# Second norm in place, transposes ahead of the Strassen sums, four gate/up products among them, fixed engine orders and ordered down loads

## The chip, the cores and the metric

The kernel runs on one core of one Trainium2 chip. The metric is device time in microseconds (us), median of several runs. Engines: PE (TensorE), DVE (VectorE), ACT (ScalarE), POOL (GpSimd) and SP (SyncE, which here only issues DMAs). All data are float32; a matmul operand is split into a high and a low part (float32r), and a product is the sum of three matmuls: high x high, high x low, low x high.

## The reference

One encoder layer on 1024 tokens of width 1024, with a hidden width of 2816. The Hyena mixer up to `y` is not touched.

```python
def rmsnorm(x, g):
    return x * lax.rsqrt(jnp.mean(x * x, axis=-1, keepdims=True) + RMS_EPS) * g

def swiglu(x, w_gate, w_up, w_down):
    return (jax.nn.silu(x @ w_gate) * (x @ w_up)) @ w_down

mixed = y @ w_out + b_out            # end of hyena_mixer(rmsnorm(x, norm_mix))
x = x + mixed
x = x + swiglu(rmsnorm(x, norm_ffn), w_gate, w_up, w_down)
return rmsnorm(x, norm_final)
```

## The kernel before

The tokens stand in eight tiles `x1[0..7]` of 128 tokens by 1024 channels. Four stages matter here.

**Out projection** (`out_mm`, L535). Blocks are done in pairs (m, m+4), first the left 512 output columns of all pairs (`po00` to `po03`), then the right 512 (`po10` to `po13`): 24 matmuls of 128x512 for a block and half. DVE adds the result onto `x1` (L551), and POOL adds the bias `bo` to the whole tile (L628).

**Second norm** (`norm2`, L570). For a pair, ACT squares both tiles (L576), DVE works out the reciprocal root in five tiny steps around an ACT square root (L133 to L138) and scales into a new tile `xm` (L579), and POOL's queue stores `x1` to DRAM (`X1D`, L559). gate/up are Strassen-Winograd products of 2x2 blocks, so DVE forms the sums of token and channel halves (`tt`, L588 to L591); PE transposes the four quarters and the sums (`tpa` to `tpd`, L598), 28 transposes of 128x128 a pair; ACT and DVE split the result into the operands `u2`, `T1`, `T2` and `T3`.

**gate/up** (`pair`, `unit`, `product`, L677). 11 pairs of a gate and an up unit; a unit has 7 products of 12 matmuls, named a, f, g, e, b, d, c, with right operands B11, T2, T3, T1, B21, T4, B22. Its weights come in two SP loads (`wgr`, `wur`). The hidden values and their sums (`g`, `sx`) are stored in `HD[0..6]` by POOL's queue; those of the last pair are "held" and stored by SP.

**Down product** (`product2`, L808). Seven products p1, p5, p6, p3, p7, p2, p4 of 132 matmuls. `operands` loads hidden blocks (`hrp`, POOL's queue), splits them into `hop`, and splits the weights `wd` into `wop`. Three slots of `hop` and `wop` take turns; one of each is the slot of `g` (tag `inv`) and of `sx` (`whl0`). DVE forms the weight sums `t1` (L856), `t2` (L861, L834) and `t4` (L867). Then come the last norm and the output stores.

The Tile framework puts the instructions of every engine in order by a simulated time line; a tile waits for its tag's slot, and a DMA from SP waits for its lane (eight of them).

Of the kernel before, what the change touches and what calls it, by code (L numbers as in the profile page):

```python
# [73 lines left out]
def hyena_ffn_kernel(ctx: ExitStack, tc: tile.TileContext, a: dict, out: bass.AP):  # L74
# [462 lines left out]
    def out_mm(pt, h, js):  # L537
        for k in range(NB):
            for q, j in enumerate(js):
                th, m = divmod(j, 4)  # L540
                for ti, (yi, wi) in enumerate(TERMS):
                    T.matmul(  # L542
                        pt[:, q * 512 : (q + 1) * 512],
                        u2[yi][th][:, k, m * P : (m + 1) * P],
                        wos[h][k // 2][wi][:, k % 2, :],
                        start=(k == 0 and ti == 0),
                        stop=(k == NB - 1 and ti == len(TERMS) - 1),
                    )
        for q, j in enumerate(js):
            d = x1[j][:, h * 512 : (h + 1) * 512]  # L550
            V.tensor_tensor(d, d, pt[:, q * 512 : (q + 1) * 512], ALU.add)  # L551

# [18 lines left out]
    def norm2(m):  # L571
        js = PAIRS[m]
        xm = slot("whl0", f"xm{m}", (2, 1024))
        sq = small(f"sq{m}", 2, tag="sq", bufs=2)
        for q, j in enumerate(js):
            S.activation(xm[:, q], x1[j], AF.Square, accum_out=sq[:, q : q + 1])  # L576
        rs = rstd_of(sq, 2, f"rq{m}")
        for q, j in enumerate(js):
            V.scalar_tensor_tensor(xm[:, q], x1[j], rs[:, q : q + 1], gffn, ALU.mult, ALU.mult)  # L579
# [1 line left out]
        if m == 0:
            t_op("T1", "ab_g", ("gg0",))
            t_op("T2", "cr", ("fwd01",))
            t_op("T3", "whl1", ("hs", "wt"))
        b11, b21 = xm[:, 0, 0:512], xm[:, 0, 512:1024]
        b12, b22 = xm[:, 1, 0:512], xm[:, 1, 512:1024]
        tt = slot("inv", f"tt{m}", (3, 512))
        V.tensor_tensor(tt[:, 0], b12, b11, ALU.subtract)  # L588
        V.tensor_tensor(b12, b22, b12, ALU.subtract)
        V.tensor_tensor(tt[:, 1], b12, b11, ALU.add)  # L590
        V.tensor_tensor(tt[:, 2], b21, tt[:, 1], ALU.subtract)  # L591
        ms = slice(m * P, (m + 1) * P)

        def turn(nm, srcs):
            pt = cv_psum(f"{nm}{m}")
            for i, src in enumerate(srcs):
                for k in range(4):
                    T.transpose(  # L598
                        pt[:, i * 512 + k * P : i * 512 + (k + 1) * P],
                        src[:, k * P : (k + 1) * P],  # L600
                        ident,
                    )
            return pt

        def whole(pt, th):
            split(u2[0][th][:, :, ms], u2[1][th][:, :, ms], pt.rearrange("p (k m) -> p k m", k=NB))

        def part(pt, i, nm):
            src = pt[:, i * 512 : (i + 1) * 512].rearrange("p (k m) -> p k m", k=4)
            hi, lo = tops[nm]  # L610
            S.copy(hi[:, :, ms], src)
            n = 4 // len(lo)
            for x, l in enumerate(lo):
# [1 line left out]
                V.tensor_tensor(l[:, :, ms], src[:, ks], hi[:, ks, ms].bitcast(F32), ALU.subtract)
# [9 lines left out]
    for m in range(4):  # L625
        out_mm(po[m], 0, PAIRS[m])
        for j in PAIRS[m]:
            G.tensor_tensor(x1[j], x1[j], bo, ALU.add)  # L628
# [22 lines left out]
    def unit(i, w, nm):  # L651
        raw = []
        for kh in range(2):
            r = slot(RAW[n_raw[0] % 4], f"{nm}r{i}{kh}", (4, 256))
# [34 lines left out]
        V.tensor_tensor(s1, a21, a22, ALU.add)
# [6 lines left out]
        product(pd, "e", s1, "T1", True)
        product(pa, "b", a12, "B21", False)
        V.tensor_tensor(s4, a12, s2, ALU.subtract)
        return (pa, pd, dc_, uu), (
            lambda: product(pc, "d", a22, "T4", False),  # L700
            lambda: product(pd, "c", s4, "B22", False),
        )

    def quads(un, rest, out):
        pa, pd, dc_, uu = un
        V.tensor_tensor(out[:, 2], uu[:, 2], pd, ALU.add)
        for f in rest:
            f()
        u2b = uu[:, 1:2].broadcast_to([P, 2, 512])
        V.tensor_tensor(  # L710
            out[:, 0:2], u2b, dc_.rearrange("p (q c) -> p q c", q=2), ALU.add
        )
# [217 lines left out]
```

## Time and profile before

| | us |
|---|---|
| median of 3 runs (1321.77 to 1322.64) | 1322.37 |
| the profiled execution | 1314.3 |
| its span | 1312.5 |
| PE busy in the span | 1193.7 |
| DVE busy | 928.7 |
| ACT busy | 435.2 |
| POOL busy | 342.7 |

The profile is of one execution. Its span runs from the first to the last instruction. An idle time in brackets stands ahead of an instruction and names what ended it.

### The profile page before, as it was taken

The numbers are of one execution on the slowest core, as the hardware profiler recorded it, in microseconds if no ns is written. First come the engines' busy times: TensorE is split into PE (matmuls) and PEld (weight loads), VectorE is DVE, ScalarE is ACT, GpSimd is POOL, SyncE is SP. The second block draws the span as 40 slices with busy tenths as digits, with TensorE's granted clock in tenths as the row PEclk, the third lists the DMA queues.
The fourth block names the chain that finished last, engine by engine and source line by source line (L and its number), as shares of the span: only waits on it lengthen the run. The fifth ranks groups of instructions, "written<-read, shape, count | busy, mean of one in ns | idle before, by whom it ended". The sixth has DMA issues, their size and how long they took to land.

```text
span 1312.5 us, 14959 instructions
## 1 busy us (share of the span) xinstructions
PE 1193.7 (91%) x5726; PEld 987.1 (75%) x5726; DVE 928.7 (71%) x1342; ACT 435.2 (33%) x665; POOL 342.7 (26%) x311
## 2 busy tenths in 40 slices
PE   3899989998999778993999999999999967999996
PEld 3688878787888667883788888888888746778875
DVE  5546999989999997367576566666657553945567
ACT  6434332333333141124332333232333321424542
POOL 0023855755754581600010010110001100000100
PEclk9999999999999888996899999999999988999999
DMA  9343231331242353141132233333232595333332
GB/s 280 79 91 89 50 80 32 73 100 37 56 103 50 115 191 98 42 151 48 48 103 90 89 105 113 104 106 109 91 96 96 192 379 191 89 88 88 96 121 96
DMA packets 88808, 139.71 MB, mean 106 GB/s; under 512 B 6559, under 2 KB 57887, under 8 KB 88609
## 3 DMA queue, kind: packets, MB, share of 16 engines
q1 hardware_dynamic: 72929, 83.44, 20.0%
q0 software_dynamic: 15808, 55.32, 14.6%
q8 instruction: 45, 0.74, 0.2%
q14 instruction: 26, 0.21, 0.0%
HBM read 94.43 MB, written 31.72 MB: 96 GB/s over the span
## 4 chain that ended last, share of the span: by engine, by line
PE 62%; DVE 25%; DMA 6%; issue 3%; POOL 2%; ACT 2%; SPq 0%; DVEq 0%; POOLq 0%; ACTq 0%
PE wgdc L677 9%; PE wudc L677 9%; PE z L111 8%; PE bx L808 7%; PE wgab L677 7%; PE wuab L677 7%; PE po L542 5%; PE by L808 3%; PE bz L808 2%; DMA wd<-in_ffn_w_down_dram 2%; DVE ss L438 2%; DVE l L383 1%; DVE vz L309 1%; DVE x L309 1%; DMA whl<-wt 1%
## 5 line engine op out<-in xcount | busy, mean ns | idle before, releaser
L111 PE MATMUL z<-uh,whl 128*128 128x512 f32 x768 | 223.3, 404 | 12.2 <-DVE x L309 3.7
L111 PEld LDWEIGHTS z<-uh,whl 128*128 128x128 f32 x768 | 145.6, 193 | 45.0 <-ACT uh L100 3.8
L808 PE MATMUL bx<-wop,hop 128*128 128x512 f32 x528 | 130.2, 403 | 21.8 <-ACT wop L100 13.0
L808 PEld LDWEIGHTS bx<-wop,hop 128*128 128x128 f32 x528 | 100.8, 193 | 49.1 <-ACT wop L100 14.2
L111 PE MATMUL z<-ul,whl 128*128 128x512 f32 x384 | 128.0, 404 | 0.0
L559 POOL DMA_DIRECT2D hd<-g x40 | 21.5, 540 | 373.0 <-DVE g L727 246.2
L101 DVE TENSOR_TENSOR hop<-hrp,hop 128x1024 fp32r<-128x1024 f32 (+1 forms) x42 | 47.5, 1133 | 57.9 <-ACT hop L100 57.9
L542 PE MATMUL po<-wohl,uh 128*128 128x512 f32 x256 | 84.4, 411 | 1.7 <-POOL wohl L101 1.7
L111 PEld LDWEIGHTS z<-ul,whl 128*128 128x128 f32 x384 | 73.6, 193 | 15.9 <-issue 0.5
L559 POOL DMA_DIRECT2D hrp<-hd x42 | 22.3, 531 | 223.4 <-DVE hop L101 179.1
L100 ACT CAST hop<-hrp 128x1024 fp32r<-128x1024 f32 (+1 forms) x42 | 40.8, 976 | 102.5 <-PE bx L808 69.0
L808 PE MATMUL by<-wop,hop 128*128 128x512 f32 x264 | 63.4, 394 | 0.8 <-DVE wop L101 0.5
L542 PEld LDWEIGHTS po<-wohl,uh 128*128 128x128 f32 x256 | 49.9, 197 | 13.4 <-POOL wohl L101 1.9
L808 PEld LDWEIGHTS by<-wop,hop 128*128 128x128 f32 x264 | 49.2, 188 | 13.5 <-DVE wop L101 2.0
L393 PE MATMUL pg<-hw,fwd 128*128 128x128 f32 x256 | 49.6, 277 | 7.7 <-DVE hw L381 7.1
L542 PE MATMUL po<-wohl,ul 128*128 128x512 f32 x128 | 51.8, 407 | 1.4 <-DVE ul L101 1.4
L165 POOL DMA_DIRECT2D whl<-wt x24 | 20.9, 871 | 122.3 <-ACT whl L164 122.3
L392 PE MATMUL pg<-hw,fwd 128*128 128x128 f32 x256 | 49.7, 276 | 0.0
L393 PEld LDWEIGHTS pg<-hw,fwd 128*128 128x128 f32 x256 | 39.3, 193 | 8.6 <-DVE hw L381 7.3
L163 ACT CAST whl<-wt 128x1024 fp32r<-128x1024 f32 x24 | 25.0, 1043 | 56.5 <-PE z L111 33.2
L101 DVE TENSOR_TENSOR wop<-wd,wop 128x512 fp32r<-128x512 f32 x55 | 36.2, 686 | 6.2 <-ACT wop L100 4.5
L392 PEld LDWEIGHTS pg<-hw,fwd 128*128 128x128 f32 x256 | 39.4, 193 | 0.3
(661 smaller groups left out, 2972.1 us busy)
## 6 DMA issues: line engine op xcount, KB each, us to landing
hrp<-hd POOLq DMA_DIRECT2D x35, 512.0 KB, 3.9
wt<-in_hy_w_in_dram SPq DMA_DIRECT2D x24, 512.0 KB
whl<-wt POOLq DMA_DIRECT2D x24, 512.0 KB, 4.5
wgr<-in_ffn_w_gate_dram SPq DMA_DIRECT2D x22, 512.0 KB
wur<-in_ffn_w_up_dram SPq DMA_DIRECT2D x22, 512.0 KB
wd<-in_ffn_w_down_dram SPq DMA_DIRECT2D x44, 256.0 KB
hd<-g POOLq DMA_DIRECT2D x40, 256.0 KB, 2.5
hd<-sx POOLq DMA_DIRECT2D x30, 256.0 KB, 2.6
```

The lines of the kernel that those rows point to most:

```text
L100: S.copy(hi, src)
L101: (eng or V).tensor_tensor(lo, src, hi.bitcast(F32), ALU.subtract)
L111: T.matmul(pt[:, h * 512 : (h + 1) * 512], w[wi], u2[ui][h][:, k, :], start=first and ti == 0, stop=last and ti == len(TERMS) - 1,)
L163: S.copy(whl[:, 0], wt)
L309: V.scalar_tensor_tensor(o, i, w, o, ALU.mult, ALU.add)
L392: T.matmul(o, fwd[r][:, j, :], hw[:, j, 0, :], start=True, stop=False)
L393: T.matmul(o, fwd[2 * r][:, jj, :], hw[:, jj, 1, :], start=False, stop=True)
L438: V.tensor_tensor(ss[:, 1], gg[:, 0], gg[:, 1], ALU.subtract)
L542: T.matmul(pt[:, q * 512 : (q + 1) * 512], u2[yi][th][:, k, m * P : (m + 1) * P], wos[h][k // 2][wi][:, k % 2, :], start=(k == 0 and ti == 0),
L559: G.dma_start(dst, src)
L677: T.matmul(pt, t[:, wi, k, :], b(k)[ui], start=first and k == 0 and ti == 0, stop=k == 3 and ti == len(TERMS) - 1, skip_group_check=not first,
L808: T.matmul(pt, ho[:, hi_, x, q * P : (q + 1) * P], wo_[:, wi, x, :], start=fresh and first and x == 0 and ti == 0, stop=last and x == n - ...
```

## The change

It has five parts.

1. The bias is no longer added by POOL's arithmetic: eight DMAs from POOL's queue add it onto `x1` in memory as each tile is loaded.
2. The left half of each block is squared when it is added (`x1_half`). SP stores each half in place of POOL's whole tile. The right half goes block by block in the order 0, 4, 1, 5, 2, 3, 6, 7. `normed` scales `x1[j]` in place, which has to follow its store.
3. `turned` transposes the normed block itself, eight transposes, 64 in all. The sums are taken afterwards from PSUM (`top_left`, `top_sums`), and three of the splits go to POOL.
4. Products a and b of both units of pair 0 stand between the last transposes, with operands split by ACT and POOL (`pre`, `pg`, `pu`). PE, DVE and ACT take the written order there.
5. SP issues in written order from the pair loop on. The down product's weight sums are formed in place (`less`), with one operation each for p5, p6, p7 and p4.

In the program's order on PE this is the stretch around the last transposes, before; the names are tile (`tp…`, `wgab`) and its operands:

```order
L598 MATMUL tpd1_4016<-ident_65,tt1_3979 128x128 x4
L598 MATMUL tpd1_4016<-ident_65,xm1_3964 128x128 x4
L598 MATMUL tpa2_4098<-ident_65,xm2_4078 128x128 x8
L598 MATMUL tpb2_4109<-ident_65,tt2_4093 128x128 x4
L598 MATMUL tpb2_4109<-ident_65,xm2_4078 128x128 x4
L598 MATMUL tpc2_4123<-ident_65,tt2_4093 128x128 x4
L598 MATMUL tpd2_4130<-ident_65,tt2_4093 128x128 x4
L598 MATMUL tpd2_4130<-ident_65,xm2_4078 128x128 x4
L598 MATMUL tpa3_4212<-ident_65,xm3_4192 128x128 x8
L677 MATMUL wgab0_4262<-uh0_61,wga0_4264 128x512
```

and in the change, on PE at block 2's transposes, between matmuls of the out projection:

```order
L549 MATMUL po14_4032<-wohl13_3570,uh0_61 128x512 x2
L549 MATMUL po14_4032<-wohl13_3570,ul0_63 128x512
L602 MATMUL tp2_4133<-ident_65,x12_3535 128x128 x8
L549 MATMUL po16_4158<-wohl10_3555,uh1_62 128x512 x2
L549 MATMUL po16_4158<-wohl10_3555,ul1_64 128x512
```

Before, the transposes of pair 2 and the first of pair 3 stand in a row with no other matmul between them; now each block's eight stand behind the next block's 24 matmuls.

On ACT, in the change, these rows follow block 5's sums (`jq` is the square of a half, `rq` the square root, `pre` the early operands of pair 0):

```order
L100 CAST uh_62<-tp_4057 128x4x128
L100 CAST pre<-wgr_4096 128x512
L100 CAST pre<-wur_4100 128x512
L563 ACTIVATE jq_4143,sq_3590<-x_3538 128x512
L590 ACTIVATE rq_4146<-rq_4146 128x1
L610 CAST uh_61<-tp_4133 128x8x128
L611 COPY x_3535<-tp_4133 128x1024
```

The two casts of loaded weights stand ahead of the square of block 3 (`x_3538`); the second of them reads the up unit's load `wur`.

On SP, around the held stores of the last pair (`hd`), before:

```order
L97 DMA wd9_7137<-in_ffn_w_down_dram 128x512 x2
L97 DMA hd1_3570<-g10_6875 128x512
L97 DMA hd3_3572<-g10_6875 128x512
L97 DMA wd9_7137<-in_ffn_w_down_dram 128x512 x2
L97 DMA y1t_7138<-xd0_3576 128x512
L97 DMA y1t_7138<-xd1_3577 128x512
L97 DMA y1t_7138<-xd2_3578 128x512
L97 DMA y1t_7138<-xd3_3579 128x512
L97 DMA wd1_7131<-in_ffn_w_down_dram 128x512
L97 DMA hd4_3573<-sx10_7125 128x512
L97 DMA wd3_7133<-in_ffn_w_down_dram 128x512
L97 DMA hd6_3575<-g10_6875 128x512
```

and in the change:

```order
L97 DMA wd7_7167<-in_ffn_w_down_dram 128x512 x2
L97 DMA wd9_7168<-in_ffn_w_down_dram 128x512 x2
L97 DMA hd0_3575<-g10_6906 128x512
L97 DMA hd1_3576<-g10_6906 128x512
L97 DMA hd3_3578<-g10_6906 128x512
L97 DMA hd4_3579<-sx10_7156 128x512
L97 DMA hd5_3580<-sx10_7156 128x512
L97 DMA hd6_3581<-g10_6906 128x512
L97 DMA hd2_3577<-sx10_7156 128x512
L97 DMA wd0_7161<-in_ffn_w_down_dram 128x512
```

The held stores stood among the loads of `wd` and of the residual (`y1t`), near the end of them; now they stand together behind the first eleven loads of `wd`.

The core of the diff:

```diff
-    bo = slot("hs", "bo")
-    load(bo, a["hy_b_out"].partition_broadcast(P)[:, 0, :])
+    bo = a["hy_b_out"].partition_broadcast(P)[:, 0, :]
     for j in range(NB):
         t = slot(x1_tags[j], f"x1{j}")
         load(t, xv[:, j, :])
+        G.dma_start(t, bo, accum_op=ALU.add)
...
+    def x1_half(j, h, o):
+        c = slice(h * 512, (h + 1) * 512)
+        V.tensor_tensor(x1[j][:, c], x1[j][:, c], o, ALU.add)
+        S.activation(
+            slot("junk", f"jq{j}{h}", (512,)), x1[j][:, c], AF.Square, accum_out=sq2[j][:, h : h + 1]
+        )
+        load(X1D[j][:, c], x1[j][:, c])
...
-    def norm2(m):
...
-        for q, j in enumerate(js):
-            V.scalar_tensor_tensor(xm[:, q], x1[j], rs[:, q : q + 1], gffn, ALU.mult, ALU.mult)
-            store(X1D[j], x1[j])
...
-        whole(turn("tpa", (b11, b21)), 0)
-        pt = turn("tpb", (tt[:, 1], b12))
-        part(pt, 0, "T2")
-        part(pt, 1, "T3")
-        pt = turn("tpc", (tt[:, 0],))
-        part(pt, 0, "T1")
-        whole(turn("tpd", (tt[:, 2], b22)), 1)
...
+    def normed(j):
...
+        for h in range(2):
+            d = x1[j][:, h * 512 : (h + 1) * 512]
+            V.scalar_tensor_tensor(d, d, r0, gffn[:, h * 512 : (h + 1) * 512], ALU.mult, ALU.mult)
+
+    def turned(j):
+        pt = cv_psum(f"tp{j}")
+        for k in range(NB):
+            T.transpose(pt[:, k * P : (k + 1) * P], x1[j][:, k * P : (k + 1) * P], ident)
+        return pt.rearrange("p (k m) -> p k m", k=NB)
...
+    def top_left(m, pt):
+        ms = cols_of(m)
+        S.copy(u2[0][0][:, :, ms], pt)
+        S.copy(x1[m].rearrange("p (k m) -> p k m", k=NB), pt)
+        V.tensor_tensor(u2[1][0][:, :, ms], pt, u2[0][0][:, :, ms].bitcast(F32), ALU.subtract)
+
+    def top_sums(m, pt):
...
+        S.copy(t3, b12)
+        V.tensor_tensor(t1, b12, left[:, 0], ALU.subtract)
+        V.tensor_tensor(t2, b22, t1, ALU.subtract)
+        V.tensor_tensor(t3, b22, t3, ALU.subtract)
+        part("T2", t2, V)
+        V.tensor_tensor(t4, left[:, 1], t2, ALU.subtract)
+        part("T3", t3, G)
+        part("T1", t1, G)
+        split(u2[0][1][:, 0:4, ms], u2[1][1][:, 0:4, ms], t4, G)
+        split(u2[0][1][:, 4:8, ms], u2[1][1][:, 4:8, ms], b22)
...
+    def w_early(t, src):
+        split(t[:, 0], t[:, 1], src, G)
+        return t
...
+    with tc.manual_schedule(
+        engines={mybir.EngineType.PE, mybir.EngineType.DVE, mybir.EngineType.Activation}
+    ):
+        for n, j in enumerate(seq):
...
+            for k in range(NB):
+                out_mm(o, 1, j, k)
...
+            if 1 <= n <= 6:
+                turn(seq[n - 1])
+            x1_half(j, 1, o)
+            if n == 6:
+                post(3)
+            normed(j)
+            if 1 <= n <= 5:
+                post(seq[n - 1])
+            if n == 4:
+                ug, uu_ = Unit(0, wg, "wg"), Unit(0, wu, "wu")
+                pre = slot("whl0", "pre", (2, 2, 4, P), F32R)
+                for x, u in enumerate((ug, uu_)):
+                    w_early(pre[:, x], u.a11)
...
+        ug.sums(G)
+        ug.p1(pre[:, 0])
+        ug.p1_out()
+        pg = w_early(slot("fwd2", "pg", (2, 4, P), F32R), ug.a12)
+        turn(6)
+        uu_.p1(pre[:, 1])
+        post(6)
+        pu = w_early(slot("xz", "pu", (2, 4, P), F32R), uu_.a12)
+        uu_.p1_out()
+        turn(7)
+        ug.p2(pg)
+        post(7)
+        uu_.p2(pu)
+        ug.early = {"f": w_op("wg0f", ug.s[:, 1])}
...
+    ctx.enter_context(tc.manual_schedule(engines={mybir.EngineType.SP}))
...
-    product2("p5", by, 4, t1, True, into(by, 1, 1))
-    product2("p6", bx, 5, t2, False, into(bx, 0, 1))
+    product2("p5", by, 4, less(B12, B12, B11), True, into(by, 1, 1))
+    product2("p6", bx, 5, less(B12, B22, B12), False, into(bx, 0, 1))
...
-    product2("p7", bx, 6, wq(B12), False, into(bx, 1, 1, lambda q: square(4 + q, 1)))
+    product2("p7", bx, 6, less(B11, B12, B11), False, into(bx, 1, 1, lambda q: square(4 + q, 1)))
...
-    product2("p4", bx, 3, t4, False, into(bx, 1, 0, lambda q: scale(4 + q, square(4 + q, 0))), 3)
+    product2("p4", bx, 3, less(B21, B21, B12), False, into(bx, 1, 0, lambda q: scale(4 + q, square(4 + q, 0))), 3)
```

More of the change, by code (lines that the diff above doesn't have):

```diff
@@ L569, in t_op @@
         tops[nm] = (hi, lo)
-    def norm2(m):
[L572 to L579, printed above, removed]
-            store(X1D[j], x1[j])
[L581 to L609, printed above, removed]
@@ L610, in part @@
+    def top_sums(m, pt):
+        ms = cols_of(m)
+        tt = slot("inv", f"tt{m}", (4, 4, P))
+        left = x1[m].rearrange("p (i k m) -> p i k m", i=2, k=4)
+        t3, t2, t1, t4 = (tt[:, i] for i in range(4))
+        b12, b22 = pt[:, 0:4], pt[:, 4:8]
+        def part(nm, src, eng):
             hi, lo = tops[nm]
@@ L696, in unit @@
[L696 to L712, printed above, removed]
@@ L714, in hyena_ffn_kernel, with p1, p1_out, p2 @@
-    wg, wu, wd = a["ffn_w_gate"][0], a["ffn_w_up"][0], a["ffn_w_down"][0]
+        def p1(u, t=None):
+            u.product(u.pa, "a", u.a11, "B11", True, t)
+        def p1_out(u):
+            S.copy(u.uu[:, 0], u.pa)
+        def p2(u, t=None):
+            u.product(u.pa, "b", u.a12, "B21", False, t)
+        def sums(u, eng):
+            eng.tensor_tensor(u.s[:, 0], u.a21, u.a22, ALU.add)
+            eng.tensor_tensor(u.s[:, 1], u.s[:, 0], u.a11, ALU.subtract)
+        def sum3(u):
+            V.tensor_tensor(u.s[:, 2], u.a11, u.a21, ALU.subtract)
@@ new lines, in sum4, with middle @@
+        def sum4(u):
+            V.tensor_tensor(u.s[:, 3], u.a12, u.s[:, 1], ALU.subtract)
+        def middle(u, early=False):
+            t = u.early if early else {}
+            u.product(u.pb, "f", u.s[:, 1], "T2", True, t.get("f"))
+            V.tensor_tensor(u.uu[:, 1], u.uu[:, 0], u.pb, ALU.add)
+            if not early:
+                u.sum3()
+            u.product(u.pc, "g", u.s[:, 2], "T3", True, t.get("g"))
+            V.tensor_tensor(u.uu[:, 2], u.uu[:, 1], u.pc, ALU.add)
+            u.product(u.pd, "e", u.s[:, 0], "T1", True, t.get("e"))
@@ new lines, in end @@
+        def end(u, out, early=False):
+            if not early:
+                u.sum4()
+            V.tensor_tensor(out[:, 2], u.uu[:, 2], u.pd, ALU.add)
+            u.product(u.pc, "d", u.a22, "T4", False)
+            u.product(u.pd, "c", u.s[:, 3], "B22", False)
+            u2b = u.uu[:, 1:2].broadcast_to([P, 2, 512])
+            V.tensor_tensor(out[:, 0:2], u2b, u.dc.rearrange("p (q c) -> p q c", q=2), ALU.add)
+    def w_early(t, src):
+        split(t[:, 0], t[:, 1], src, G)
+        return t
@@ L716, in hyena_ffn_kernel, with pair @@
     held = []
-    def pair(i):
+    def pair(i, ug=None, uu_=None):
         put = store if i < NP - 1 else lambda *x: held.append(x)
         g = slot("inv", f"g{i}", (4, 512))
-        un, rest = unit(i, wg, "wg")
-        S.activation(g[:, 0], un[0], AF.Silu)
-        quads(un, rest, g[:, 1:4])
-        S.activation(g[:, 1:4], g[:, 1:4], AF.Silu)
-        un, rest = unit(i, wu, "wu")
+        early = ug is not None
+        if not early:
+            ug = Unit(i, wg, "wg")
+            ug.begin()
+            ug.p1()
+            ug.p1_out()
+            ug.sums(V)
+            ug.middle()
+            ug.p2()
+        else:
+            ug.middle(True)
+        S.activation(g[:, 0], ug.pa, AF.Silu)
+        ug.end(g[:, 1:4], early)
+        S.activation(g[:, 1:4], g[:, 1:4], AF.Silu)
+        if not early:
+            uu_ = Unit(i, wu, "wu")
+            uu_.begin()
+            uu_.p1()
+            uu_.p1_out()
+            uu_.sums(V)
+            uu_.middle()
+            uu_.p2()
+        else:
+            uu_.middle(True)
```

163 lines of the change are left out of this document (89 added, 74 removed).

## The prediction

> **What bounds the kernel now.** I read the page's head first, then the stretches of equal length with each engine's busy time and the granted TensorE clock.
>
> ```profile
> span 1312.5 us, 14959 instructions
> PE 1193.7 (91%) x5726; PEld 987.1 (75%) x5726; DVE 928.7 (71%) x1342; ACT 435.2 (33%) x665; POOL 342.7 (26%) x311
> ```
>
> ```profile
> 580.00:600.00 20.00, 15.44 (x77) 12.50 (x75) 16.68 (x29) 4.43 (x9) 2.12 (x4) 0.91 0.45 159
> 600.00:620.00 20.00, 5.83 (x28) 4.85 (x28) 13.69 (x26) 9.33 (x17) 0.00 (x0) 0.59 0.08 26
> 620.00:640.00 20.00, 15.72 (x65) 12.23 (x66) 13.78 (x20) 6.98 (x11) 0.00 (x0) 0.74 0.10 27
> 700.00:800.00 100.00, 100.00 (x436) 81.57 (x435) 65.78 (x96) 29.42 (x46) 10.77 (x20) 1.00 0.32 104
> 1060.00:1080.00 20.00, 14.16 (x50) 10.47 (x48) 12.49 (x15) 5.18 (x8) 1.60 (x3) 0.83 1.05 386
> 1080.00:1100.00 20.00, 8.54 (x31) 6.90 (x32) 5.69 (x8) 4.83 (x8) 1.05 (x2) 0.74 0.81 315
> 1118.85:1160.00 41.15, 38.37 (x159) 29.32 (x160) 34.56 (x51) 15.79 (x23) 4.78 (x9) 1.00 0.35 103
> 1260.00:1300.00 40.00, 37.86 (x161) 29.49 (x160) 32.58 (x73) 17.59 (x33) 1.07 (x2) 1.00 0.23 80
> ```
>
> Columns: stretch, length, then busy time (and count) of PE, PEld, DVE, ACT and POOL, clock, DMA share, GB/s. PE bounds almost everything: in the gate/up loop it is busy 100.00 of 100 us, 436 products, 0.2294 us each. It has two holes: the transition from the out projection to the gate/up loop (580 to 640), and the start of the down product (1060 to 1100). There the clock falls too. The change touches both, and leaves the loop's 12-matmul products alone.
>
> **The transition as it is.** The chain of waits gives a rate, PE's own waits the rest:
>
> ```profile
> 525.44 40.02 PE po L542 x172
> ```
> ```profile
> 565.29 1.03 PE L598 MATMUL tpa<-ident,xm 128*128 128x128 f32 x8
> 636.17 0.60 PE L598 MATMUL tpd<-ident,tt 128*128 128x128 f32 x4
> 636.60 0.60 PE L598 MATMUL tpd<-ident,xm 128*128 128x128 f32 x4
> 636.96 0.47 PE L677 MATMUL wgdc<-T3h,wgg 128*128 128x512 f32 x1
> ```
> ```profile
> PE tpa L598 <- DVE xm L579: 11.7, 2, 5.8
> PE tpd L598 <- DVE T1l L615: 4.7, 2, 3.3
> PE tpb L598 <- DVE tt L590: 3.4, 1, 3.4
> ```
>
> An out-projection matmul costs 40.02 / 172 = 0.2327 us. 94 of the second half's 192 stand ahead of the first transposes at 565.29, so that half begins at T0 = 565.29 - 94 x 0.2327 = 543.4. Eight warm transposes cost 2 x 0.43 = 0.87 us (starts 636.17 and 636.60). By 636.96 PE has done 192 matmuls, 24 of gate 0 and 112 transposes: 44.7 + 5.5 + 12.2 = 62.4 us of work in 93.6. The other 31 us are waits on DVE's norm chain and a cold clock.
>
> **The transition as it will be.** Up to the first product that uses T2, PE has the 192 matmuls (44.7), 64 transposes instead of 112 (64 x 0.87 / 8 = 7.0) and 48 products of pair 0 (48 x 0.2294 = 11.0): 62.7 us. The waits between them come from this chain for each token block, with these prices:
>
> ```profile
> L551 DVE TENSOR_TENSOR x<-x,po 128x512 f32<-128x512 f32 x10 | 6.4, 684 | 17.2 <-PE po L542 17.2
> L579 DVE SCALAR_TENSOR_TENSOR xm<-x,rq,gffn 128x1024 f32<-128x1024 f32 x8 | 9.9, 1282 | 0.2
> L576 ACT ACTIVATE xm<-x 128x1024 f32<-128x1024 f32 x6 | 6.3, 1054 | 0.0
> 602.59 0.16 DVE L136 SCALAR_TENSOR_TENSOR rq<-rq 128x2 f32<-128x2 f32 x1
> 602.78 0.16 DVE L137 TENSOR_TENSOR rq<-rq 128x2 f32<-128x2 f32 x1
> ```
>
> Add 0.68, half a square with its read about 0.75, six tiny steps at a 0.195 pitch with the square root between about 1.4, two half scalings about 1.4: 4.3 us. One block's 24 matmuls take 5.6, so each chain is covered while nothing else stands in its queue. Four places are not covered. (a) Block 3: the second ACT cast of `pre` stands ahead of the block's square and waits for a weight load. It can issue only when x1[1]'s slot is free, and takes about 4 us:
>
> ```profile
> 777.21 0.37 SPq L97 DMA_DIRECT2D wur<-in_ffn_w_up_dram  x1
> 781.06 0.69 DVE L689 TENSOR_TENSOR wus<-wur,wur 128x512 f32<-128x512 f32 x1 [0.66 <-DMA wur<-in_ffn_w_up_dram]
> ```
>
> Stepping the fixed orders with these durations, turn 3 waits 3.8 us. (b) The split of `pu` stands on POOL behind four splits of m = 2: 4.2. (c) The first T2 product waits 1.9 for its weight split behind the last sums. (d) Block 5 waits 0.9, and `pg` 0.9. Together 11.7.
>
> But POOL now shares this stretch with DVE, and that costs DVE:
>
> ```profile
> 472.73 4.38 POOL L101 TENSOR_TENSOR ul<-yr,uh 128x512 fp32r<-128x512 f32 x3
> 474.48 1.49 DVE L328 TENSOR_TENSOR s7ct<-s7ab 128x256 f32<-128x256 f32 x1
> 484.07 0.41 DVE L331 TENSOR_TENSOR s7ab<-s7ab 128x256 f32<-128x256 f32 x1
> ```
>
> The same DVE form takes 0.41 us alone and 1.49 beside a POOL split (4.38 / 3 = 1.46). Each POOL split thus holds a DVE instruction with two SBUF inputs for about 1.1 us. Letting the two exclude each other in the stepping lifts the waits to 1.3 + 5.2 + 0.6 + 4.7 + 3.2 = 15.0 us; I take that. The Trainium skill ("SBUF — State Buffer", Who interferes with whom) says that such a DVE instruction and a GpSimd instruction that reads SBUF exclude each other whole; the trace agrees, 1.49 against 0.41. That rule speaks against this change's moves to POOL; without it the waits would be 11.7.
>
> The bias moves from POOL additions to eight accumulating DMAs. They are issued ahead of T0, so I cost them at nothing:
>
> ```profile
> L628 POOL TENSOR_TENSOR x<-x,bo 128x1024 f32<-128x1024 f32 x8 | 18.9, 2409 | 7.1 <-DVE x L551 7.1
> whl<-wt POOLq DMA_DIRECT2D x24, 512.0 KB, 4.5
> hd<-sx POOLq DMA_DIRECT2D x30, 256.0 KB, 2.6
> hrp<-hd POOLq DMA_DIRECT2D x35, 512.0 KB, 3.9
> ```
>
> Eight of them in a line at 4.5 us would be 36; the first out-projection half lasts 45, and if that cover fails, the first adds wait some microseconds. The in-place scaling must wait until its half's store has landed. No row shows such a store from SP; 2.6 us (a 256 KB store by POOL) hides behind the 3 us from add to scaling, and the upper bound of 5 adds 11.
>
> A cold clock comes on top: after 5.2 us of idle, the matmuls from 1065.60 on run at half clock for about 5.5 us, a loss of 2.75.
>
> ```profile
> 1064.00:1067.00 3.00, 1.41 (x3) 1.16 (x4) 3.00 (x4) 1.54 (x2) 0.47 (x1) 0.50 1.05 387
> 1070.00:1073.00 3.00, 3.00 (x13) 2.38 (x13) 0.50 (x1) 0.00 (x0) 0.00 (x0) 0.88 1.03 392
> ```
>
> Waits (a) and (b) are of that length; part of the second loss falls into wait (c). I take 4 us, from 0 to 7.5. The Trainium skill ("TensorE: Matmul & The Clock Gate", The two states you'll see) puts the warm-up at about 3.4 us of busy time, an estimate of 1.7 us lost per gap and 3.4 for two; the trace's clock takes longer to return.
>
> The first T2 product so starts at 543.4 + 62.7 + 15.0 + 4 = 625.1. The 1800 remaining products cost 412.9, plus 1.5 for small waits: the loop ends at 1039.5.
>
> **The start of the down product.**
>
> ```profile
> 1059.97 0.40 PE L677 MATMUL wudc<-uh,wuc 128*128 128x512 f32 x1
> 1065.60 13.80 PE L808 MATMUL bx<-wop,hop 128*128 128x512 f32 x48 [5.23 <-ACT hop L100]
> 1091.46 16.83 PE L808 MATMUL bx<-wop,hop 128*128 128x512 f32 x66 [12.06 <-ACT wop L100]
> 1090.79 1.14 ACT L100 CAST wop<-wd 128x512 fp32r<-128x512 f32 x2 [2.15 <-DMA hd<-sx]
> 1079.74 0.32 SPq L97 DMA_DIRECT2D hd<-sx  x1
> 1083.60 0.98 SPq L97 DMA_DIRECT2D hd<-sx  x2
> ```
>
> The loop ends at 1059.97 + 0.40 = 1060.4 now, so the transition is worth 20.9. From there to 1118.85 stand 158 down matmuls (48 and 66 in the two rows, 44 behind them), 36.2 us of work at 0.2294: 22.2 are lost. The 12.06 is a slot: the third operand pair takes the slots of `g10` and `sx10`, whose stores SP issues only between 1079.74 and 1084, among the weight loads. In the new order the held stores stand behind the eleven B11 loads and ahead of all else. They go as soon as DVE has made the sums, about 7 us after the loop's end, land by 11, and the third pair is ready at about 13, while PE needs it at about 18 (7 plus 48 x 0.2294). That hole goes. The first one stays, since the last difference (1.22), product (1.75) and low half of `hop` (1.2) still follow the last matmul, and three sums (0.6 each) now stand ahead of the second `hop`: some 6 us idle, 2.75 for the clock, 1 for its neighbours, 9.8. **Worth 12.4**, from 5 (if the hd loads from DRAM, beside weight loads at 386 GB/s, come late) to 16.
>
> **The rest of the down product.** Between 1118.85 and 1160 PE lacks 2.8 us; DVE is full there. One of the three weight sums of p6 moves to p7, 11 x 0.69 = 7.6 us out of the full stretch: worth 2.3 of the 2.8. From 1260 to 1300 PE lacks 2.1, where the 11 differences of p4 now stand earlier: 1.5.
>
> **Sum.** 20.9 + 12.4 + 2.3 + 1.5 = 37.1. The profiled execution took 1314.3 (span 1312.5 and 1.8 around it) and would take 1277.2; the runs' median is 1322.4, 8.1 above it, and I keep that gap: 1285.3.
>
> **The rivals.** *The in-place wait takes the norm chain's place*: a store that lands in 5 us, as an upper bound beside the 3.9 of a 512 KB transfer, makes turns 0, 1, 5, 2, 3 and 7 wait, 11 us in all: 1296. For it: it is a new wait on every block. Against: 256 KB by POOL lands in 2.6. *The down start stays as slow*: hd loads meet B12 loads in the full DMA stretch, and the 12.4 vanish: 1298. For it: DMA share is 1.05 there. Against: four hd loads can go ahead of the held stores. *SP's fixed order stalls the loop (slower)*: a load that waits for its slot now holds all loads behind it. If each of the last 21 units loses 3 us, 63 us are lost and the time is 1348; it decides from 37.1 / 21 = 1.8 us a unit. For it: the scheduler's order now leaves DVE only 0.66 of waiting for `wur`. Against: the slots are freed in the order in which the loads are written, and the loop loses nothing now. *The holes only change their place* (the out projection's wait goes, but the fixed DVE order stalls PE at pair 0, and the down start too): 1322, no change.
>
> **How the numbers follow.** Forecast as worked, 1270 to 1292: 0.62. In-place wait 0.15, down start unchanged 0.11, both 0.04 (1309), no change 0.03, SP stall 0.05. Faster by over 0.2%, 2.6 us, which is about what a measurement of this kernel can tell from no change: 0.92; within it 0.03; slower 0.05. The range takes in the two single failures with some microseconds of the cold clock above them; below, waits of 11.7 (3.3 less), no cold clock (4 less), 16 for the down start (3.6 more) and all of 2.8 and 2.1 at the end (1.1 more) make 1273, and a load that lands in 3 us instead of 4 takes another 1 to 2: 1270 to 1304.
>
> **What would show it.** Right: PE waits of 4 to 6 us at turn 3 and at the `pu` product, none over 2 at the other turns; DVE instructions above 1 us beside POOL splits; the first T2 product about 82 us after the second half begins; the loop still at 436 products in 100 us; one hole of about 6 us at the down start and no 12.06. Wrong: turns that wait for SP's stores, gate/up products that wait for loads, or a second hole before the third operand pair.

## The result and the profile after

The changed kernel takes 1294.03 us, the median of four runs (1292.27 to 1294.42). The kernel before, timed beside it, takes 1322.51 (1321.77 to 1322.82). The ratio is 0.9783, with a 95% interval from 0.9766 to 0.98: faster by 2.2%. The prediction said 1285, from 1270 to 1304.

The profiled executions tell another size. That of before took 1314.3 and that of the change 1294.2, so the traces differ by 20.4 us of span and the medians by 28.5. Where the other 8 come from turned out to be the main finding.

The span from the page of the changed kernel, and then the same kind of stretches as before (length, busy time and count of PE, PEld, DVE, ACT and POOL, granted clock, DMA share, GB/s):

```profile
span 1292.1 us, 14966 instructions
```

```profile
580.00:600.00 20.00, 18.45 (x87) 14.55 (x86) 12.56 (x26) 8.75 (x18) 8.17 (x9) 1.00 0.36 115
600.00:620.00 20.00, 15.86 (x65) 12.52 (x64) 11.54 (x26) 8.49 (x17) 5.67 (x5) 0.83 0.09 31
620.00:640.00 20.00, 16.27 (x60) 11.70 (x58) 15.79 (x21) 10.49 (x19) 11.58 (x10) 0.83 0.11 29
700.00:800.00 100.00, 100.00 (x436) 81.64 (x435) 64.90 (x94) 29.72 (x47) 10.81 (x20) 1.00 0.31 107
1060.00:1080.00 20.00, 19.44 (x76) 15.80 (x77) 13.60 (x19) 7.42 (x12) 2.66 (x5) 0.88 1.00 362
```

PE is busy 50.58 us from 580 to 640, where it was 36.99, and 19.44 from 1060 to 1080, where it was 14.16. The gate/up loop still does 436 products in 100 us, so SP's fixed order does not stall it. The clock falls to 0.83 over forty microseconds of the transition.

PE's own waits from 500 to 660 (engine, line, releaser; total, times, longest), and then PE's timeline at the places on which the prediction rests (start, duration, idle time ahead in brackets):

```profile
PE po L549 <- DVE ul L101: 3.8, 1, 3.8
PE tp L602 <- issue: 3.7, 1, 3.7
PE po L549 <- DVE x L562: 3.5, 3, 2.0
PE wu0ab L688 <- POOL pu L101: 2.6, 1, 2.6
PE wu0ab L688 <- ACT wu0f L100: 2.3, 1, 2.3
...
PE wu0ab L688 <- ACT wu0u L701: 0.9, 1, 0.9
PE tp L602 <- PE po L549: 0.5, 1, 0.5
```

```profile
558.52 0.73 PE L549 MATMUL po<-wohl,uh 128*128 128x512 f32 x2 [2.00 <-DVE x L562]
...
565.77 1.03 PE L602 MATMUL tp<-ident,x 128*128 128x128 f32 x8
...
633.09 0.63 PE L688 MATMUL wg0ab<-T2h,wg0f 128*128 128x512 f32 x1
...
642.04 0.50 PE L688 MATMUL wu0ab<-T2h,wu0f 128*128 128x512 f32 x1 [2.31 <-ACT wu0f L100]
...
1052.61 0.39 PE L688 MATMUL wu10dc<-uh,wu10c 128*128 128x512 f32 x1
1060.56 28.39 PE L912 MATMUL bx<-wop,hop 128*128 128x512 f32 x114 [7.56 <-ACT hop L100]
...
1098.19 0.39 PE L912 MATMUL by<-wop,hop 128*128 128x512 f32 x1
1099.32 0.73 PE L912 MATMUL by<-wop,hop 128*128 128x512 f32 x2 [0.74 <-ACT wop L100]
1100.87 20.01 PE L912 MATMUL by<-wop,hop 128*128 128x512 f32 x86 [0.82 <-DVE wop L101]
...
1132.12 0.74 PE L912 MATMUL bx<-wop,hop 128*128 128x512 f32 x2 [0.96 <-ACT wop L100]
```

The holes that were foreseen to stay are there (turn 3 and `pu` in the first view, one hole ahead of the down product in the second), and the 12.06 us hole is gone. The longest wait of the first view, 3.8 us for `ul` early in the out projection, was not foreseen; e2 bears on it. To see what moved, I cut every trace at the same marks: `pn`, the start of the last row of L450, near the end of the mixer's convolution (such a row stands once for each of its eight blocks); the first transposes of the second norm; the first product with T2; E, the end of the last gate/up matmul (here 1052.61 + 0.39 = 1053.00); the end of the span.

| us | start to pn | pn to transposes | to T2 | to E | E to end | span |
|---|---|---|---|---|---|---|
| before, profiled | 485.6 | 79.7 | 67.4 | 427.7 | 252.1 | 1312.5 |
| change, profiled | 492.8 | 72.9 | 67.3 | 419.9 | 239.1 | 1292.1 |
| change as predicted, from the same pn | 485.6 | 69.0 | 70.5 | 414.4 | 235.9 | 1275.4 |

The transposes stand at another place in each kernel's order, so the middle columns compare the last two rows only. The prediction and the trace are 16.7 us apart: 7.2 ahead of `pn`, in a part that the change does not touch, 6.3 from there to E, 3.2 behind E.

### The profile page after: what moved, and what is told of

Read it like the earlier page. It is cut to its first block, busy times and chain, and to the rows that moved or that the text cites. A ratio compares the mean times of both kernels' runs of the same rounds, so it can differ in the third digit from the quotient of the medians.

```text
span 1292.1 us, 14966 instructions
## 1 busy us (share of the span) xinstructions
PE 1191.2 (92%) x5678; PEld 984.5 (76%) x5678; DVE 937.3 (73%) x1360; ACT 443.4 (34%) x697; POOL 353.0 (27%) x325
## 4 chain that ended last, share of the span: by engine, by line
PE 48%; DVE 4%; issue 2%; ACT 1%; DMA 1%; POOL 0%; DVEq 0%; ACTq 0%; SPq 0%; POOLq 0%
PE bx L912 9%; PE by L912 5%; PE bz L912 2%; PE po L549 2%; PE wu7dc L688 1%; PE wg9dc L688 1%; PE wu2dc L688 1%; PE wg5dc L688 1%; PE wg4dc L688 1%; PE wu1dc L688 1%; PE wu6dc L688 1%; PE wu5dc L688 1%; PE wu0dc L688 1%; PE wg8dc L688 1%; PE wg3dc L688 1%
## 5 line engine op out<-in xcount | busy, mean ns | idle before, releaser
L912 PE MATMUL bx<-wop,hop 128*128 128x512 f32 x528 | 127.1, 398 | 10.8 <-ACT hop L100 7.6
L101 DVE TENSOR_TENSOR wop<-wd,wop 128x512 fp32r<-128x512 f32 x77 | 50.7, 686 | 6.6 <-ACT wop L100 6.6
L165 POOL DMA_DIRECT2D whl<-wt x24 | 21.0, 874 | 122.8 <-ACT whl L164 122.8
L100 ACT CAST wop<-wd 128x512 fp32r<-128x512 f32 x77 | 44.2, 616 | 16.6 <-DMA wd<-in_ffn_w_down_dram 6.9
L393 PEld LDWEIGHTS pg<-hw,fwd 128*128 128x128 f32 x256 | 39.3, 193 | 8.3 <-DVE hw L381 7.0
L163 ACT CAST whl<-wt 128x1024 fp32r<-128x1024 f32 x24 | 25.0, 1043 | 56.0 <-PE z L111 32.1
```

The source lines that it names most:

```text
L100: S.copy(hi, src)
L101: (eng or V).tensor_tensor(lo, src, hi.bitcast(F32), ALU.subtract)
L163: S.copy(whl[:, 0], wt)
L165: G.dma_start(whl[:, 1].bitcast(F32), wt, accum_op=ALU.add)
L393: T.matmul(o, fwd[2 * r][:, jj, :], hw[:, jj, 1, :], start=False, stop=True)
L912: T.matmul(pt, ho[:, hi_, x, q * P : (q + 1) * P], wo_[:, wi, x, :], start=fresh and first and x == 0 and ti == 0, stop=last and x == n - ...
```

## The experiments

The theories: (A) the 7.2 us are a race of two engines in the untouched convolution, which the profiled execution of before happened to win; against it, the change itself delays the convolution. (B) the accumulating bias loads cost the 3.9 us ahead of the transposes; against it, PE's own order. (C) POOL's splits hold DVE; (D) the early operands `pre` make the wait at turn 3; (E) the down hole is a late load slot; against it, DVE's chain; (F) SP's order alone makes the gain at the down start. Single runs have a run of the kernel before beside them (1313.14 for e1 to e4, 1314.53 for e5 to e8). The profiled execution of each run, with its marks:

| run | time | start to pn | pn to E | E to end |
|---|---|---|---|---|
| change | 1294.2 | 492.8 | 560.2 | 239.1 |
| e1_before_again | 1322.02 | 495.7 | 571.9 | 252.7 |
| e2_no_bias | 1295.99 | 494.1 | 557.3 | 242.8 |
| e3_dve_splits | 1294.04 | 492.9 | 560.3 | 239.0 |
| e4_late_pre | 1297.51 | 493.0 | 560.6 | 242.1 |
| e6_before_sp_order | 1307.88 | 492.2 | 573.9 | 239.7 |
| e7_fwl_pool | 1280.92 | 481.4 | 560.5 | 237.2 |
| e8_bias_mix | 1296.46 | 491.3 | 561.1 | 242.2 |
| e9_changed_again | 1289.25 | 487.8 | 560.6 | 239.1 |
| e10_fwl_pool_timed | 1281.31 | 483.0 | 557.4 | 239.1 |
| e11_before_fwl_pool | 1308.39 | 480.2 | 570.9 | 255.6 |
| e12_combined | 1283.05 | 480.2 | 558.6 | 242.2 |

(e5 has down products ahead of E, so its marks do not compare; it took 1295.17.)

### e1: the kernel before once more, unchanged

> The kernel before, profiled again. Its runs gave 1322.5 us and its profiled execution 1314.3. Theory (a race in the convolution stage): the low-part subtraction at L366 near 231 us starts after POOL's row of three operations, takes about 10 us instead of 0.42, and the span is about 1320 instead of 1312.5; everything behind it stands about 7 us later. Rival (the 8 us are spread, or lie outside the span): L366 takes 0.4 us and the span stays near 1312 while the time reads 1322.

It took 1322.02, while the run beside it took 1313.14: the same kernel on the same chip. The timeline around 231 us shows one place where such runs part. `fwl` is the low half of a filter weight, one DVE subtraction of two SBUF tiles (L366). First the profiled execution of before, rows of DVE and POOL:

```profile
231.20 0.42 DVE L366 TENSOR_TENSOR fwl<-fw,fwh 128x256 fp32r<-128x256 f32 x1
...
231.81 4.91 POOL L436 TENSOR_TENSOR gg<-ss,gg 128x2048 f32<-128x2048 f32 x1
```

the same place in e1:

```profile
233.24 9.92 DVE L366 TENSOR_TENSOR fwl<-fw,fwh 128x256 fp32r<-128x256 f32 x1
...
233.38 4.89 POOL L436 TENSOR_TENSOR gg<-ss,gg 128x2048 f32<-128x2048 f32 x1
```

and in the changed kernel:

```profile
231.63 10.25 DVE L366 TENSOR_TENSOR fwl<-fw,fwh 128x256 fp32r<-128x256 f32 x1
...
232.07 4.91 POOL L436 TENSOR_TENSOR gg<-ss,gg 128x2048 f32<-128x2048 f32 x1
236.66 2.63 POOL L405 TENSOR_TENSOR sig<-vz,xz 128x1024 f32<-128x1024 f32 x1
238.97 2.62 POOL L437 TENSOR_TENSOR ss<-cr 128x1024 f32<-128x1024 f32 x1
```

The operation that takes 0.42 us takes about 10 when POOL's row of three begins at nearly the same time: in the change it ends at 241.88, when the third of them does (241.59). By the recorded starts DVE wins where it is 0.61 us ahead of POOL, and loses 0.44 and 0.14 ahead.

Not all of the lost time lasts. At the L450 row ahead of this place the change is 0.3 us later than the profiled execution of before (217.81 against 217.54), at the next 5.8 (274.27 against 268.50), at the third 7.0 (323.00 against 315.95), and at the last 7.2. So of the 9.8 us by which the instruction is longer some 5.5 last, and most of the rest comes behind the next L366, which takes 1.76 us in the change and 0.42 before. In e1 the part up to `pn` is 10.1 longer than in the profiled execution of before, but 2.0 of that stand ahead of this place (233.24 against 231.20). Theory A fits, and the change is not needed for the delay: e6, also without the rest of the change, has 10.20 us at this place.

### e7 and e10: the changed kernel with L366 on POOL

```diff
-        V.tensor_tensor(fwl, fw, fwh.bitcast(F32), ALU.subtract)
+        G.tensor_tensor(fwl, fw, fwh.bitcast(F32), ALU.subtract)
```

> The changed kernel with the filter's low-part subtraction (L366) on POOL instead of DVE. Theory (a race with POOL's row of operations costs 7 to 10 us at 231 us): no DVE instruction of about 10 us near 231, the second to last convolution mark (the pn matmul now at 492.8) comes 5 us or more earlier, time 1284 to 1289. Rival (POOL's queue delays it as much, or the time comes back later): within 3 us of 1294.

> The changed kernel with L366's subtraction on POOL, timed. Theory: with the race gone it reads 1280 to 1283 in every execution. Rival (the one run of 1280.9 was a fortunate one): it spreads over more than 5 us or reads above 1288.

e7 took 1280.92, less than the 1284 to 1289 that were expected, and the part up to `pn` 481.4 instead of 492.8. Timed in three rounds (e10): 1281.2 (1280.6 to 1281.66); against before (1321.24, seven runs) the ratio is 0.9696, interval 0.9677 to 0.9716. The group row of e10 (busy us, mean ns, idle time ahead):

```profile
L366 POOL TENSOR_TENSOR fwl<-fw,fwh 128x256 fp32r<-128x256 f32 x8 | 6.5, 810 | 24.7 <-ACT fwh L365 24.7
```

On POOL the eight cost 0.81 us each in the mean. This is the fastest version of the study, and faster than both kernels. With L366 off DVE the delay at 231 us is gone, and with e1 and e9, where one kernel loses the race once and wins it once, A is shown.

But the edit gains more than the race. The part up to `pn` (481.4 and 483.0) is also shorter than in the executions that won at 231, the profiled one of before (485.6) and e9 (487.8). The rest stands at a second place of the same kind, the addition to two columns at L310. DVE and POOL in the change:

```profile
432.76 9.35 DVE L310 TENSOR_TENSOR vz<-vz,edge 128x2 f32<-128x2 f32 x1
...
432.62 2.72 POOL L435 TENSOR_TENSOR cr<-ss,gg 128x1024 f32<-128x1024 f32 x1
...
437.28 4.80 POOL L436 TENSOR_TENSOR gg<-ss,gg 128x2048 f32<-128x2048 f32 x1
```

and DVE in e10:

```profile
429.32 2.19 DVE L310 TENSOR_TENSOR vz<-vz,edge 128x2 f32<-128x2 f32 x1
```

This addition is held 9.35 us in the change, 9.68 in the profiled execution of before and 9.59 in e9, through three POOL operations, and 2.19 in e10, through one. PE's wait behind it (`pg` for DVE's `hw`) is 6.8, 7.1, 7.0 and 0.7 us. Between the L450 rows around the race (217.81 and 274.27 in the change) e10 is 6.0 us shorter, and between those around L310 (420.88 and 481.19) 7.4; elsewhere ahead of `pn` it loses 3 to 4 of these again. What lets it go after one operation in e10 was not tried.

### e9 and e11: how wide the race is, and what the change is worth without it

e9 is the changed kernel as it was; e11 is the kernel before with the edit of e7.

> The changed kernel once more, beside runs of the kernel before on the same chip. Theory (a race in the convolution that both kernels carry): the kernel before reads 1313 to 1315 in executions in which L366 starts ahead of POOL's row and 1322 in others; the changed one reads 1292 to 1295 in all where it loses, and 1285 to 1287 where it wins. Rival (the 9 us belong to the kernel before alone): the changed kernel never reads below 1291 and no L366 of about 10 us stands in it when it does.

> The kernel before with L366's subtraction on POOL. Theory (the race is shared, so that without it the change is worth what the stages show, 14 us up to the loop's end and 13 behind it): 1307 to 1311 in every execution, 27 to 29 above the changed kernel with the same edit. Rival (the edit helps the changed kernel only): 1314 or 1322 as before.

e9: 1289.25, 1294.96, 1292.45, 1299.62, median 1293.7, ratio 0.9794 (0.9758 to 0.983). On this chip one kernel spreads over 10 us. Its profiled run won at 231 and was held at L310, as two DVE rows show:

```profile
230.75 0.69 DVE L366 TENSOR_TENSOR fwl<-fw,fwh 128x256 fp32r<-128x256 f32 x1
...
427.14 9.59 DVE L310 TENSOR_TENSOR vz<-vz,edge 128x2 f32<-128x2 f32 x1
```

It was the fastest of the four, above the 1285 to 1287 expected of a won race, and still 8 us above e10: 4.8 of these lie ahead of `pn`, where L310 is held, and 3.2 from there to E. e11 took 1310.93 (1308.39 to 1313.18), 0.9921 of before (0.9897 to 0.9946). With L366 on POOL in both, the change is worth 1310.93 - 1281.2 = 29.7 us, near the 28.5 of the medians and not the 20.4 of the two traces. e10's four runs lie within 1.1 us, e11's within 4.8: before has other sources of spread that this edit does not remove.

### e2: without the bias

```diff
-        G.dma_start(t, bo, accum_op=ALU.add)
```

This leaves `b_out` out of the result.

> The changed kernel without the eight accumulating DMAs: the bias b_out is left out of the output. Theory (the accumulation lands late: an add waited 8.0 us for it and PE 2.0 at 558.5): the first adds wait for PE only, the 2.0 us wait goes, and the gate/up loop begins 3 to 5 us earlier against the start of the convolution's end; time about 1290. Rival (the waits were covered): no PE wait goes and the time stays within 1 us of 1294.

DVE's row of the change at the sixth of the left-half additions, and how long the accumulating loads take from issue to landing:

```profile
553.83 0.69 DVE L562 TENSOR_TENSOR x<-x,po 128x512 f32<-128x512 f32 x1 [8.01 <-DMA x<-in_hy_b_out_dram]
```

```profile
L530 POOL DMA_DIRECT2D x<-in_hy_b_out_dram x8: 857/872/1222, 489.8 to 544.6; - x8
...
DMA to landing us min/median/max: 4.9/7.7/9.1
```

In e2 DVE's 8.01 us wait is gone, PE's 2.00 behind it falls to 0.78, and the transposes come 68.7 us after `pn` instead of 72.9. B is shown in sum: 4.3 us. But only 1.2 of them stand at this place. Another 2.7 are the wait for `ul` at 503.55, 3.84 us in the change and 1.12 in e2. In the change POOL waits for the plain load of `x` before it issues an accumulating one, and its next splits so begin beside DVE's `ul`:

```profile
497.38 0.87 POOL L530 DMA_DIRECT2D x<-in_hy_b_out_dram  x1 [6.64 <-DMA x<-in_x_dram]
497.94 5.00 POOL L101 TENSOR_TENSOR wohl<-wo,wohl 128x1024 fp32r<-128x1024 f32 x2
...
497.87 5.63 DVE L101 TENSOR_TENSOR ul<-yr,uh 128x512 fp32r<-128x512 f32 x1
```

In e2 this `ul` takes 1.73 us. By these rows the loads cost more by holding up POOL's queue than by landing late. The expected time was missed all the same. By T2 the lead is 4.8; by E 2.9 (560.2 to 557.3); and behind E 3.7 are lost, so the run was no faster. The hole at the down start is longer here than the 7.56 of the change:

```profile
1060.17 10.12 PE L911 MATMUL bx<-wop,hop 128*128 128x512 f32 x31 [8.76 <-ACT hop L100]
```

### e8: three of the biases added by POOL

```diff
+    bt = slot("hs", "bt")
+    load(bt, bo)
...
-        G.dma_start(t, bo, accum_op=ALU.add)
+        if j in (3, 6, 7):
+            G.tensor_tensor(t, t, bt, ALU.add)
+        else:
+            G.dma_start(t, bo, accum_op=ALU.add)
```

> The changed kernel with the bias of the last loaded tiles 3, 6 and 7 added by POOL arithmetic instead of an accumulating DMA. Theory (a late accumulation, 9 us behind the load it must follow, holds the adds): DVE's 8.0 us wait for it falls below 2 and the first transposes come 2 to 4 us earlier against the mark pn; time about 1291. Rival (POOL arithmetic holds DVE as much): the first transposes do not move.

1296.46. DVE's 8 us wait is gone, but the transposes gain only 0.9 against `pn`, since PE now has another wait, of 6.5 us early in the out projection (in the change the wait there is 3.8):

```profile
PE po L554 <- DVE x L309: 6.5, 1, 6.5
```

So this mix moves the wait to an earlier place. A cheaper bias is not had that way.

### e3: the three splits back on DVE

```diff
-        part("T3", t3, G)
-        part("T1", t1, G)
-        split(u2[0][1][:, 0:4, ms], u2[1][1][:, 0:4, ms], t4, G)
+        part("T3", t3, V)
+        part("T1", t1, V)
+        split(u2[0][1][:, 0:4, ms], u2[1][1][:, 0:4, ms], t4)
```

> The changed kernel with the three splits of the sums (T3, T1, T4) on DVE instead of POOL. Theory (POOL holds DVE instructions with two SBUF inputs, and is late for pu): no DVE instruction over 1 us beside them, the pu product's wait of 2.6 us goes, but DVE has 4 x 4 more operations of 0.4 to 0.6 us: the first T2 product comes at most 3 us earlier or up to 3 later. Rival (no contention; POOL is free help): the first T2 product comes 5 us or more later, with turn waits at every block, and the time is about 1299.

1294.04, as the change. The group row of DVE's first weight sum, in the change and then in e3:

```profile
L711 DVE TENSOR_TENSOR wg0s<-wgr 128x512 f32<-128x512 f32 x1 | 1.8, 1764 | 0.0
```

```profile
L711 DVE TENSOR_TENSOR wg0s<-wgr 128x512 f32<-128x512 f32 x1 | 0.7, 685 | 0.0
```

```profile
PE wu0ab L688 <- ACT wu0u L701: 2.8, 1, 2.8
```

POOL's splits do hold DVE (1.76 us against 0.69), but at the `pu` product PE then waits 2.8 for `wu0u` instead of 2.6 for `pu` and 0.9 for `wu0u`. From the transposes to T2 it takes 65.9 instead of 67.3, and by E nothing is left. C is right as a mechanism and worth at most 1.4 us, where the prediction put 3.3.

### e4: the second early cast behind block 3's square

```diff
             normed(j)
+            if n == 5:
+                w_early(pre[:, 1], uu_.a11)
...
-                for x, u in enumerate((ug, uu_)):
-                    w_early(pre[:, x], u.a11)
+                w_early(pre[:, 0], ug.a11)
```

> The changed kernel with the second early cast (pre, up unit) put behind the square of block 3. Theory (turn 3 waits since the square stands behind a cast that waits for its load): the PE wait at turn 3, 3.7 us, falls to under 1.5, and the time by 2 to 4 us. Rival (turn 3 waits for DVE, which POOL holds): the wait stays above 3 us.

1297.51. PE's waits in e4:

```profile
PE po L549 <- DVE x L562: 4.5, 3, 2.4
...
PE tp L602 <- issue: 2.0, 1, 2.0
```

The wait at turn 3 falls from 3.7 to 2.0 and the waits of `po` rise from 3.5 to 4.5; to T2 it takes 67.1 instead of 67.3. D names the wait rightly, but it covers others: what is late next takes its place.

### e5: the held `hrp` loads into slots that are free earlier

```diff
-    HRAW = ("xz", "s1", "hs", "wt")
+    HRAW = ("hs", "wt", "xz", "s1")
```

> The changed kernel with the first two hidden loads of the down product in the slots hs and wt (free after the last T3 product) instead of xz and s1 (free after the last product of all). Theory (the 7.6 us hole is a hidden load that POOL can issue only when the last gate/up product has freed its slot, and that takes 6 us among the weight loads): the hole falls to 3 to 5 us. Rival (the hole is DVE's chain of last difference, product and low half, as predicted): it stays at 6 to 8 us.

In the change the first down product waits for the second `hop`. Its ACT cast waits for a load that POOL can only issue when the last gate/up product has freed the slot (20.53 us of idle ahead of it):

```profile
1053.29 0.53 POOL L544 DMA_DIRECT2D hrp<-hd  x1 [20.53 <-PE wu10dc L688]
...
1059.46 1.04 ACT L100 CAST hop<-hrp 128x1024 fp32r<-128x1024 f32 x1 [4.13 <-DMA hrp<-hd]
```

With the other slots (e5) PE shows

```profile
1060.49 1.47 PE L912 MATMUL bx<-wop,hop 128*128 128x512 f32 x4 [3.12 <-ACT hop L100]
1064.31 6.62 PE L912 MATMUL bx<-wop,hop 128*128 128x512 f32 x20 [2.36 <-DVE hop L101]
```

and two more waits, of 1.34 and 1.21 us for `wop`, by 1074.22. One wait of 7.56 becomes four, 8.0 in all, and the time is 1295.17. The load's slot ended the hole, so E is right about what came last; DVE's chain stands right behind it, so the slot alone is worth nothing.

### e6: the kernel before with SP's order fixed

```diff
+    ctx.enter_context(tc.manual_schedule(engines={mybir.EngineType.SP}))
     for i in range(NP):
```

> The kernel before with SP's written order from the pair loop on, and nothing else of the change. Theory (the held stores' place alone makes the second hole): the 12 us wait for wop goes, and from the loop's end to the span's end it takes about 240 us as in the changed kernel instead of 252. Rival (the other parts, in-place sums and shorter DVE work, give the 13 us): it stays above 247.

1307.88, with 1314.53 beside it. From E to the end it takes 239.7, against 252.1 in the profile of before and 239.1 in the change. PE's timeline in e6:

```profile
1066.83 11.69 PE L809 MATMUL bx<-wop,hop 128*128 128x512 f32 x48 [0.71 <-ACT hop L100]
1082.52 17.64 PE L809 MATMUL bx<-wop,hop 128*128 128x512 f32 x65 [4.01 <-ACT wop L100]
```

The 12.06 us wait for the third operand pair is 4.01, and the 5.23 ahead of the first product, which the expectation did not name, is 0.71. One line gives nearly the whole gain behind E (12.5 of 13.0 us), though not by the same holes: in the change the second is gone and the first is 7.56. The regrouped weight sums add next to nothing to it. F is shown.

### e12: L366 on POOL, e3 and e8 together

> The changed kernel with L366 on POOL, the three splits of the sums on DVE, and the bias of tiles 3, 6 and 7 added by POOL arithmetic. Theory (each removes a wait that PE sees: 1.4 us to the first T2 product by the splits, 1.0 by the bias): 1278 to 1280, 2 us under L366 alone. Rival (the waits pass on to the gate/up units and the down start): within 1 us of L366 alone.

1286.12 (1283.05 to 1289.17), ratio 0.9742 (0.9712 to 0.9772): 4.9 slower than L366 alone, which neither the expectation nor its rival had. By the medians the two other edits cost time: from E to the end it takes 242.2, as in e2, e4 and e8, against 239.1, and the runs spread over 6 us again. The 3 us stand at two places. In these four runs the wait ahead of the first down matmul is 8.3 to 8.8 us, not 7.56, and the 108 matmuls from the 289th on take 27.6, not 26.0: behind the same two short waits, 0.96 and 0.82, the clock falls to 0.55 (e2, 1135 to 1138) where it is 1.00 in the change. What decides between the two was not found.

## Why the prediction was right, and where it was not

**The time and the sum.** 1294.03 lies in the range, 9.0 above the point, but also 2 above the 1292 at which the forecast as worked was to end; it is in the range through the margin for single failures. The medians differ by 28.5 where the sum said 37.1. Against the two traces the sum was 6.3 too good between `pn` and E and 3.2 behind E, 9.5 together. Up to the first T2 product it came out, 140.2 us from `pn` for 139.5, but by luck: the bias loads cost 3.9 that stood at nothing, and the waits were 3.2 shorter. So of the 6.3, 5.5 lie behind T2.

**"8.1 above it, and I keep that gap."** Right by size without knowing why, and so by luck. The profiled execution of before had won the race at L366. Its timed runs, of which there is no trace, lie where e1 lies, which loses it, and the four runs of the change lie together with the profiled one, which loses it as well. A reader who compares the two traces alone puts the change at 20.4 us; the 7.2 that are missing arise some 250 us ahead of the first instruction that it adds, a bias load at 489.8.

**"issued ahead of T0, so I cost them at nothing."** This failed. They are issued ahead of the second half, which begins at 550.77 in the change, but the last at 544.6, and they take 4.9 to 9.1 us, median 7.7, not the 4.5 of the row that priced them; that row, `whl<-wt`, accumulates too (L165), but from SBUF. DVE waits 8.01 us for one of them, and the wait of POOL ahead of one makes PE wait 3.84 for `ul`, a path that the text did not have. e2 measures 4.3 us up to the transposes; the text had named "some microseconds" for the case that the cover fails.

**The waits up to T2, 15.0 and 4 for the clock.** The mechanisms of the two long waits were right, the sizes not. Turn 3 waits 3.7 (5.2 in the sum, 3.8 without contention), `pu` 2.6 (4.7) and block 5's turn 0.5 (1.3); the 0.6 for `pg` and the 3.2 ahead of the first T2 product are not there, and 0.9 for `wu0u` and 1.5 for `po` were not in the sum. The rows of the waits between the transposes and T2 sum to 3.7 + 2.6 + 0.9 + 0.5 + 1.5 of `po` (3.5 less the 2.0 ahead of the transposes) = 9.2. The work that the prediction counted there is 51.5 us of the 67.3, so 6.6 are left for the clock and small gaps, against 4: at a clock of 0.83, 32.1 us of busy PE from 600 to 640 lose about 5.5 (an estimate from those two rows). The sum of 19 was 3.2 too large.

**"1.5 for small waits" behind T2.** This failed: 419.9 us for 412.9 of work, so 7.0. 2.31 is the up unit's first T2 product, which waits for the ACT split of its weights; it stands nine microseconds behind the place at which the prediction had it. 0.87 and 0.78, at 1040.67 and 1047.21, are in the last pair. The other 3.0 I cannot place product by product.

**The start of the down product, 12.4.** Right in size. The timeline of before has the 158th and the 289th matmul of the down product here:

```profile
1116.17 2.22 PE L808 MATMUL by<-wop,hop 128*128 128x512 f32 x9
...
1152.20 0.74 PE L808 MATMUL bx<-wop,hop 128*128 128x512 f32 x2 [0.96 <-ACT wop L100]
```

The 158th ends at 1118.39, so the 156th at 1117.93, 57.56 after E. In the change the 156th ends at 1098.19 + 0.39, 45.58 after E. That is 12.0 gained. Of the 9.8 that were to stay lost, 45.58 - 156 x 0.2294 = 9.8 are: a longer idle time, 7.56, and a milder clock. (The 2.75 for the clock was a little high: by its own two rows the half clock lasts until about 1070.7, 5.1 us, an estimate of 2.6.) The cause was named wrongly, DVE's chain in place of the load's slot, and e5 shows DVE's chain as the next to wait for.

**The relief of DVE, 2.3 + 1.5.** This failed. Up to the start of the 289th down matmul (1132.12; before 1152.20) 12.7 are gained, at the end 13.0, so the 3.8 came to 1.0. The premise was off as well: the row by which DVE was called full has it busy for 34.56 of 41.15 us. PE's waits there are 0.74 and 0.82 in p5 and 0.96 and then another 0.82 in p6, each pair 24 matmuls behind the start of the product, for the cast and the split of a weight, and those in p6 are there in both kernels. What sets them was not tried.

**The rivals.** The in-place store makes one DVE wait, 1.06 us:

```profile
592.10 0.75 DVE L597 SCALAR_TENSOR_TENSOR x<-x,rq,gffn 128x512 f32<-128x512 f32 x1 [1.06 <-DMA xd<-x]
```

and PE does not wait for it. SP's order stalls no product of the loop, the down start did not stay as slow, and the holes did not merely move.

## What to carry to other kernels

Check whether the one profiled execution is a usual one before a sum is built on it: if it lies several microseconds off the timed runs, find the instruction whose duration differs, since two kernels may be compared in a won and in a lost race. A short two-input DVE operation beside a row of long POOL operations is such an instruction, and moving one to POOL was worth more (12.5 us of 1293.7) than any refinement of the change, though about half of that came at a second operation of this kind, which the move had not aimed at: list them all before one is moved. And a wait that is taken away is worth only its distance to the next one: in five runs (e2, e3, e4, e5, e8, each timed once) the wait that was aimed at went or shrank, and none of them was faster.
